# A decoder layer on one core: TensorE in source order through the gates, attention scores in pairs, and the adaLN sums placed elsewhere

## The chip, the core and the metric

One core of a Trainium2 chip runs the whole layer in one launch. The metric is the time of one execution in microseconds of the device. The core's engines work side by side and meet through semaphores: TensorE (PE in the profile, with PEld for its weight loads) multiplies, VectorE (DVE) and ScalarE (ACT) do element-wise work, GpSimd (POOL) a little of both, and SyncE (SP) issues the loads. Results of TensorE land in eight PSUM banks.

## The reference, cut to what matters

SEQ is 256, D_MODEL 1024, D_FF 2816, 8 heads of 64, SSM width 512. With 256 tokens there is a single MoBA block, so the attention is plain causal attention with ALiBi.

```python
ada = jax.nn.silu(c) @ w_ada[l] + b_ada[l]                # nine vectors of 1024
sh1, sc1, g1, sh2, sc2, g2, sh3, sc3, g3 = jnp.split(ada, N_ADA, axis=-1)
h = modulate(rmsnorm(x, norm_ffn1[l]), sh1, sc1)
x = x + 0.5 * g1[:, None, :] * swiglu(h, w_ffn1_in[l], w_ffn1_out[l])
h = modulate(rmsnorm(x, norm_mix[l]), sh2, sc2)
q, k, v, u, ga, gs = jnp.split(h @ w_in[l], IN_SPLITS, axis=-1)
y_att = moba_attention(q.reshape(hd), k.reshape(hd), v.reshape(hd))
y_ssm = s5_mixer(u, ...)       # diagonal complex state space, then gelu and a sigmoid gate (w_glu)
merged = (jax.nn.sigmoid(ga) * (y_att @ w_br_att[l]) + jax.nn.sigmoid(gs) * (y_ssm @ w_br_ssm[l]))
x = x + g2[:, None, :] * (merged @ w_out[l])
h = modulate(rmsnorm(x, norm_ffn2[l]), sh3, sc3)
x = x + 0.5 * g3[:, None, :] * swiglu(h, w_ffn2_in[l], w_ffn2_out[l])
return rmsnorm(x, norm_final)
```

All inputs are float32, and each weight is read once.

## The kernel before

**Weights.** Every weight matrix comes in units of 1 MB: `add_unit` and its kin list them, and SyncE's queue loads them in the order of that list into a ring `raw` of four slots (`NRAW`). The load of unit i is issued when unit i-4 has been used up. A weight unit is split in two quanta of 128x1024; ScalarE rounds a quantum to `w_hi` (L296), VectorE makes the rest, `w_lo` (L304), and a 128x128 block then takes three 256-column matmuls: hi x hi, hi x lo, lo x hi (`mm3` L327 to L329, `proj_mm` L500 to L502, and L649 in the start). A quantum is 24 matmuls. The splits run `AHEAD` = 4 quanta ahead of TensorE, in five buffers.

**The adaLN vectors.** The nine vectors v = 0 to 8 take four units each from the same ring. VectorE multiplies each half by silu(c) and adds it to `acc` (`consume_ada`, L274 and L276, two instructions a unit). When the fourth unit is in, `ada_done` queues `do_cols` on `pe_fill`, which runs four quanta later: column sums over the partitions on TensorE (L403, a 32-wide column group for each quarter), a copy to `ada_rows` by ScalarE (L408), two small matmuls with columns of the identity that turn the rows to columns (L410), and `ada_cols` on VectorE. `fill` takes one due item from `pe_fill` for each quantum. Vector 2, 4 and 3 are spread through FFN1 (`ffn_units`, one unit where `put * room < total * (n + 1)`), 5, 7 and 6 through the mixer by `MIX_ADA` (one unit behind each of the last 12 of its 14 weight units), 8 in FFN2.

**Stages of TensorE** (times of the profile): the start and the first seven FFN1 tiles to 64, FFN1 to 233, norm, q, k and v to 263, four u tiles to 274, the mixer's gates to 360, SSM gate, branches and output projection to 416, FFN2 to 600. `ssm_prep`, a generator that is advanced once a quantum in FFN1, builds the SSM's tables, with groups of four 128x128 transposes in banks 2 and 3 by turns (L896, L910, L935).

**The gates stage.** Each of the 16 gate tiles takes one quantum: 24 matmuls with the tile's bank out of 4, 5 and 6 by turns, then ScalarE's tanh. Between tiles `events` list the other work: for each head the scores `qk_mm` (L1272, L1273) with the softmax of VectorE and ScalarE behind it, one tile later `p_t` (three transposes, L1306), another tile later `pv_mm` (L1325, L1327; it does two heads at a time, in column groups 0 to 63 and 64 to 127 of one bank). `s_mm(0)` and `s_mm(1)` (L1188, 16 matmuls of 64 columns each) make the SSM's inputs from `U`, which is copied out of the u tiles' banks in 64 small copies, half of them on VectorE (L1180). The scans follow on VectorE, and `y_mm` (L1246, twelve matmuls at once, in column groups of 32) makes their outputs between the matmuls of gate 6 and later.

**What sets the order.** Some stages have TensorE's order written out (`manual_schedule`). From the u tiles through the gates a scheduler sets it by its own estimates: it may pull single instructions of the events between the matmuls of a tile. On the other engines it sets the order in any case.

**The final gain.** `final_gain` turns the last norm's gain from rows to a column with an 8x8 transpose (L1438), 30 quanta into what follows the first raw pair of FFN2.

## Time and profile before

| | us |
|---|---|
| three runs | 611.45, 613.01, 613.42 (median 613.01) |
| the profiled execution | 611.65 |
| its span in the trace | 609.5 |
| TensorE busy | 598.2 |
| VectorE busy | 456.1 |
| ScalarE busy | 326.9 |

The profile is that of one execution. Times in rows count from the start of its span; 2.15 us of the execution lie outside the span. A matmul's row has its start and its duration from issue to drained end; matmuls overlap, so what one costs in a stream is the distance between two starts. "PEclk" is the granted share of TensorE's full clock.

### The profile page before, as it was taken

The numbers are of one execution on the slowest core, as the hardware profiler recorded it, in microseconds if no ns is written. First come the engines' busy times: TensorE is split into PE (matmuls) and PEld (weight loads), VectorE is DVE, ScalarE is ACT, GpSimd is POOL, SyncE is SP. The second block draws the span as 40 slices with busy tenths as digits, with TensorE's granted clock in tenths as the row PEclk, the third lists the DMA queues.
The fourth block names the chain that finished last, engine by engine and source line by source line (L and its number), as shares of the span: only waits on it lengthen the run. The fifth ranks groups of instructions, "written<-read, shape, count | busy, mean of one in ns | idle before, by whom it ended". The sixth has DMA issues, their size and how long they took to land.

```text
span 609.5 us, 12820 instructions
## 1 busy us (share of the span) xinstructions
PE 598.2 (98%) x5328; PEld 571.3 (94%) x5328; DVE 456.1 (75%) x838; ACT 326.9 (54%) x537; POOL 25.3 (4%) x37
## 2 busy tenths in 40 slices
PE   7999999999999999999999999999999999999996
PEld 7888999999999999998987899999999999999995
DVE  2689999889867569998999859968975646445433
ACT  4445856469435445846536865447744444444434
POOL 6201010020000001000000000001000000000000
PEclk8999999999999999998999999999999999999997
DMA  9999989875969555888448836564586746745201
GB/s 278 335 312 247 362 276 368 280 263 177 317 212 343 178 172 172 312 270 284 139 140 282 276 135 208 195 221 139 208 275 209 247 168 233 249 149 200 70 2 70
DMA packets 97770, 136.70 MB, mean 224 GB/s; under 512 B 7761, under 2 KB 77474, under 8 KB 97712
## 3 DMA queue, kind: packets, MB, share of 16 engines
q1 hardware_dynamic: 97424, 135.81, 66.8%
q8 instruction: 42, 0.69, 0.5%
q14 instruction: 16, 0.13, 0.1%
q0 software_dynamic: 288, 0.07, 0.1%
HBM read 134.82 MB, written 1.05 MB: 223 GB/s over the span
## 4 chain that ended last, share of the span: by engine, by line
PE 88%; DVE 4%; DMA 4%; ACT 2%; issue 1%; POOL 0%; SPq 0%; ACTq 0%; DVEq 0%
PE bank L327 16%; PE bank L328 16%; PE bank L329 16%; PE bank L500 8%; PE bank L501 8%; PE bank L502 8%; PE bank L649 5%; DVE w_lo L304 2%; PE bank L425 1%; DMA raw<-in_w_in_dram 1%; PE bank L1246 1%; DMA raw<-in_w_ada_dram 1%; PE bank L1188 1%; DMA ssm_G<-in_w_ffn_in_dram 1%; DVE acc L276 1%
## 5 line engine op out<-in xcount | busy, mean ns | idle before, releaser
L304 DVE TENSOR_TENSOR w_lo<-raw,w_hi 128x1024 fp32r<-128x1024 f32 x168 | 204.2, 1223 | 84.2 <-ACT w_hi L296 83.8
L296 ACT CAST w_hi<-raw 128x1024 fp32r<-128x1024 f32 x168 | 174.0, 1048 | 165.5 <-PE bank L328 97.4
L327 PE MATMUL bank<-h_hi,w_hi 128*128 128x256 f32 x736 | 209.5, 285 | 0.0
L329 PE MATMUL bank<-h_hi,w_lo 128*128 128x256 f32 x736 | 207.1, 281 | 0.0
L328 PE MATMUL bank<-h_lo,w_hi 128*128 128x256 f32 x736 | 207.0, 281 | 0.0
L327 PEld LDWEIGHTS bank<-h_hi,w_hi 128*128 128x128 f32 x736 | 139.5, 190 | 3.9 <-issue 2.3
L329 PEld LDWEIGHTS bank<-h_hi,w_lo 128*128 128x128 f32 x736 | 140.0, 190 | 0.3 <-issue 0.2
L328 PEld LDWEIGHTS bank<-h_lo,w_hi 128*128 128x128 f32 x736 | 139.0, 189 | 0.1
L500 PE MATMUL bank<-a,w_hi 128*128 128x256 f32 x352 | 99.2, 282 | 0.0
L501 PE MATMUL bank<-a,w_hi 128*128 128x256 f32 x352 | 98.9, 281 | 0.0
L502 PE MATMUL bank<-a,w_lo 128*128 128x256 f32 x352 | 98.4, 280 | 0.0
L276 DVE SCALAR_TENSOR_TENSOR acc<-raw,csil,acc 128x1024 f32<-128x1024 f32 x49 | 62.8, 1281 | 7.8 <-DMA raw<-in_w_ada_dram 7.5
L500 PEld LDWEIGHTS bank<-a,w_hi 128*128 128x128 f32 x352 | 66.5, 189 | 1.0 <-issue 1.0
L502 PEld LDWEIGHTS bank<-a,w_lo 128*128 128x128 f32 x352 | 66.7, 190 | 0.0
L501 PEld LDWEIGHTS bank<-a,w_hi 128*128 128x128 f32 x352 | 66.1, 188 | 0.0
L327 PE MATMUL bank<-a,w_hi 128*128 128x258 f32 x112 | 31.9, 286 | 0.0
L328 PE MATMUL bank<-a,w_hi 128*128 128x258 f32 x112 | 31.8, 284 | 0.0
L329 PE MATMUL bank<-a,w_lo 128*128 128x258 f32 x112 | 31.5, 282 | 0.0
L649 PE MATMUL bank<-h_hi,w_hi 128*128 128x256 f32 x112 | 27.4, 294 | 0.9 <-ACT w_hi L296 0.5
L649 PE MATMUL bank<-h_lo,w_hi 128*128 128x256 f32 x112 | 27.8, 286 | 0.0
L649 PE MATMUL bank<-h_hi,w_lo 128*128 128x256 f32 x112 | 27.4, 283 | 0.0
L446 POOL TENSOR_TENSOR rstd<-rstd,mhalf 128x2 f32<-128x2 f32 x4 | 4.7, 1168 | 456.8 <-DVE rstd L445 456.8
(337 smaller groups left out, 893.0 us busy)
## 6 DMA issues: line engine op xcount, KB each, us to landing
raw<-in_w_ffn_in_dram SPq DMA_DIRECT2D x36, 1024.0 KB, 5.4
raw<-in_w_ada_dram SPq DMA_DIRECT2D x28, 1024.0 KB, 5.2
raw<-in_w_ffn_out_dram SPq DMA_DIRECT2D x22, 1024.0 KB, 5.3
raw<-in_w_in_dram SPq DMA_DIRECT2D x16, 1024.0 KB, 5.5
raw<-in_w_ada_dram SPq DMA_DIRECT2D x16, 512.0 KB, 8.1
raw<-in_w_out_dram SPq DMA_DIRECT2D x4, 1024.0 KB, 4.8
a<-in_w_ffn_in_dram SPq DMA_DIRECT2D x8, 448.0 KB, 7.1
ssm_G<-in_w_ffn_in_dram SPq DMA_DIRECT2D x4, 896.0 KB, 10.7
```

Of the source, the lines that this page charges most:

```text
L276: nc.vector.scalar_tensor_tensor(out=a, in0=r[:, k, :], scalar=cs, in1=a, op0=ALU.mult, op1=ALU.add)
L296: nc.scalar.copy(hi, r)
L304: nc.vector.tensor_tensor(out=lo, in0=r, in1=hi.bitcast(F32), op=ALU.subtract)
L327: nc.tensor.matmul(o, st[0], mv[0], start=first, stop=False)
L328: nc.tensor.matmul(o, st[0], mv[1], start=False, stop=False)
L329: nc.tensor.matmul(o, st[1], mv[0], start=False, stop=last)
L425: nc.tensor.matmul(p[q:q + 32, 0:256], csil[:, k, :], r[:, k, :], start=(k < 4), stop=(k >= 4), tile_position=(0, q))
L500: nc.tensor.matmul(mm3_o, wj[0], a[0], start=first and j % 2 == 0, stop=False)
L501: nc.tensor.matmul(mm3_o, wj[0], a[1], start=False, stop=False)
L502: nc.tensor.matmul(mm3_o, wj[1], a[0], start=False, stop=last and j % 2 == 1)
L649: nc.tensor.matmul(pb[b][:, n * S:(n + 1) * S], z[:, b * 128:(b + 1) * 128], h[hl][:, kb, :], start=(kb == 0 and n == 0 and y == 0), stop= ...
L1188: nc.tensor.matmul(S_b[f][n][:, i * 64:(i + 1) * 64], ssm["G"][n][:, 8 * f + i, :], U[:, 8 * f + i, 0:NC4], start=True, stop=True,)
```

## The change

Five things are changed.

1. **Units of `ada`.** Vector 5 joins FFN1: its 16 units are put so that the first half of the stage gets six and the second half ten, one for each weight unit. In the mixer, vector 7's four units stand behind k and u units, none behind the first four gate units, and vector 6's four behind the last four.
2. **Finishing a vector.** `do_cols` becomes `sums` (column sums, copy to `ada_rows`), then one quantum later `turn_rows` (two full 128x128 transposes instead of the two matmuls with identity columns; VectorE picks the columns it needs), then two quanta later a `spacer`, one 8x8 transpose whose result nobody reads. One more spacer stands ahead of the u tiles.
3. **TensorE's order** from the u tiles to the last gate is that of the source. `s_mm(0)` stands behind the third u tile, `s_mm(1)` behind gate 2. `y_mm` begins at gate 8.
4. **Paired scores.** `qk_mm` does two heads, on partitions 0 to 63 and 64 to 127, in banks 0 and 6, at gates 2, 5, 8 and 11; `p_t` of both follows at gates 5, 8, 11, 14 in banks 1 and 7, `pv_mm` at 7, 10, 13, 15. Gate tiles use banks 4, 5, 7 and 1 for the first four and 4 and 5 by turns from then on.
5. **Smaller moves.** `final_gain` comes 8 quanta in, not 30. `ssm_prep` starts one quantum later and uses bank 2 alone.

```diff
--- before.py
+++ after.py
@@ -31,7 +31,7 @@
 AHEAD = 4
 FILL_DELAY = 4
 PUMP = 1
-MIX_ADA = (0, 0, 1, 1, 1, 1, 1, 1, 1, 1, 1, 1, 1, 1)
+MIX_ADA = (0, 0, 1, 1, 1, 1, 0, 0, 0, 0, 1, 1, 1, 1)
 HOLD = 3
 RAWS = 2
 KTILES = 7
@@ -180,12 +180,14 @@
         total, put, room = len(spread), 0, len(units) - 5
         for n, u in enumerate(units):
             u()
-            while put < total and put * room < total * (n + 1):
+            while put < total and put * room < (
+                total * (n + 1) if total < 16 else max(12 * (n + 1), 20 * (n + 1) - 4 * room)
+            ):
                 ada_unit(*spread.popleft())
                 put += 1
 
-    ffn_units(T["w_ffn1_in"][0], T["w_ffn1_out"][0], KTILES, [(v, j) for v in (2, 4, 3) for j in range(4)])
-    mix_ada = deque((v, j) for v in (5, 7, 6) for j in range(4))
+    ffn_units(T["w_ffn1_in"][0], T["w_ffn1_out"][0], KTILES, [(v, j) for v in (2, 4, 3, 5) for j in range(4)])
+    mix_ada = deque((v, j) for v in (7, 6) for j in range(4))
 
     def mix_sprinkle(n=1):
         for _ in range(n):
@@ -385,19 +387,26 @@
 
     def ada_cols(v, p, ks):
 
-        o, b = ada[v][:, ks], bada[:, v, ks]
+        o, b, g = ada[v][:, ks], bada[:, v, ks], norm_cols[v][:, ks] if v in norm_cols else None
+        if len(p.shape) == 3:
+            o, b, g = (z if z is None else z.rearrange("p (q n) -> p q n", n=2) for z in (o, b, g))
         if v in norm_cols:
             nc.vector.scalar_tensor_tensor(out=o, in0=p, scalar=1.0, in1=b, op0=ALU.add, op1=ALU.add)
-            nc.vector.tensor_tensor(out=o, in0=o, in1=norm_cols[v][:, ks], op=ALU.mult)
+            nc.vector.tensor_tensor(out=o, in0=o, in1=g, op=ALU.mult)
         else:
             nc.vector.tensor_tensor(out=o, in0=p, in1=b, op=ALU.add)
             if v % 3 == 2:
                 nc.vector.tensor_scalar(o, o, 0.5, None, op0=ALU.mult)
 
+    def spacer():
+
+        p = bank(state["bank"])
+        nc.tensor.transpose(p[:, 0:8], rows[0], ident[0:8, 0:8])
+
     def ada_done(v):
         a = acc.pop(v)
 
-        def do_cols():
+        def sums():
             p = bank(state["bank"])
             for q in range(4):
                 nc.tensor.matmul(
@@ -406,13 +415,16 @@
                 )
             rs = sb("ada_rows", [128, 256])
             nc.scalar.copy(rs, p[:, 0:256])
+            pe_fill.appendleft((state["q"] + 1, lambda: turn_rows(rs)))
+
+        def turn_rows(rs):
+            p = bank(state["bank"])
             for n in range(2):
-                nc.tensor.matmul(
-                    p[:, 256 + n:264:2], rs[:, n * 128:(n + 1) * 128], ident[:, ::32], start=True, stop=True
-                )
-            ada_cols(v, p[:, 256:264], slice(0, KD))
-
-        pe_fill.append((state["q"] + FILL_DELAY, do_cols))
+                nc.tensor.transpose(p[:, n * 128:n * 128 + 128], rs[:, n * 128:(n + 1) * 128], ident)
+            ada_cols(v, p[:, 0:256].rearrange("p (n q c) -> p q n c", n=2, q=4)[:, :, :, 0], slice(0, KD))
+            pe_fill.append((state["q"] + 2, spacer))
+
+        pe_fill.append((state["q"] + FILL_DELAY, sums))
 
     block_sb = {}
 
@@ -889,9 +901,10 @@
         prep_ok[0] = False
         yield
         yield
+        yield
         Cc = pcs[1]
         for i in range(2):
-            p = bank(3)
+            p = bank(2)
             for j in range(4):
                 nc.tensor.transpose(
                     p[:, j * 128:(j + 1) * 128], c_raw[i][:, j].rearrange("p a b -> p (a b)"), ident
@@ -905,7 +918,7 @@
         G = [sb(f"ssm_G{i}", [128, 16, 128]) for i in range(2)]
         for i in range(2):
             for q in range(4):
-                p = bank(2 + q % 2)
+                p = bank(2)
                 for n in range(4):
                     nc.tensor.transpose(
                         p[:, n * 128:(n + 1) * 128],
@@ -916,7 +929,7 @@
                 )
                 yield
         ssm["G"] = G
-        p = bank(3)
+        p = bank(2)
         for j in range(4):
             for n in range(2):
                 for q in range(4):
@@ -1163,6 +1176,20 @@
     for t in range(2):
         nc.scalar.copy(vt[t], vb[t])
 
+    S_b = {}
+
+    def s_mm(f):
+        S_b[f] = (bank(2), bank(3))
+        for i in range(8):
+            for n in range(2):
+                nc.tensor.matmul(
+                    S_b[f][n][:, i * 64:(i + 1) * 64], ssm["G"][n][:, 8 * f + i, :],
+                    U[:, 8 * f + i, 0:NC4], start=True, stop=True,
+                )
+
+    pe_fill.appendleft((0, spacer))
+    gates = ExitStack()
+    gates.enter_context(tc.manual_schedule(engines={E_.PE}))
     U = sb("ssm_U", [128, 16, NC4 + 1])
     nc.gpsimd.memset(U[:, :, 0:1], 0.0)
     for j in range(4):
@@ -1178,17 +1205,9 @@
                     nc.scalar.copy(o, i_)
                 else:
                     nc.vector.tensor_copy(o, i_)
-
-    S_b = {}
-
-    def s_mm(f):
-        S_b[f] = (bank(2), bank(3))
-        for i in range(8):
-            for n in range(2):
-                nc.tensor.matmul(
-                    S_b[f][n][:, i * 64:(i + 1) * 64], ssm["G"][n][:, 8 * f + i, :],
-                    U[:, 8 * f + i, 0:NC4], start=True, stop=True,
-                )
+        if j == 2:
+            s_mm(0)
+
 
     Xs = {}
 
@@ -1265,12 +1284,16 @@
     ya = []
     pv_b = {}
 
-    def qk_mm(hd):
-        j, o = hd // 2, 64 * (hd % 2)
-        p = bank(0)
-        sc_b[hd] = p
-        nc.tensor.matmul(p[:, 0:128], qT[o:o + 64, j, 0:128], kT[o:o + 64, j, 0:128], start=True, stop=True)
-        nc.tensor.matmul(p[:, 128:384], qT[o:o + 64, j, 128:256], kT[o:o + 64, j, :], start=True, stop=True)
+    def qk_mm(j):
+
+        for i in range(2):
+            sc_b[2 * j + i] = bank(6 * i)
+        for c, r in ((slice(0, 128), slice(0, 128)), (slice(128, 384), slice(128, 256))):
+            for i in range(2):
+                o = 64 * i
+                nc.tensor.matmul(
+                    sc_b[2 * j + i][:, c], qT[o:o + 64, j, r], kT[o:o + 64, j, 0:r.stop], start=True, stop=True
+                )
 
     def softmax(hd):
         p = sc_b.pop(hd)
@@ -1301,7 +1324,7 @@
 
     def p_t(hd):
         e = pn.pop(hd)
-        p = bank(1)
+        p = bank((1, 7)[hd % 2])
         for n in range(3):
             nc.tensor.transpose(p[:, n * 128:(n + 1) * 128], e[:, n * 128:(n + 1) * 128], ident)
         t = sb(("silu", "act_f")[hd % 2], [128, 384])
@@ -1330,7 +1353,6 @@
             nc.scalar.copy(ya[0][:, j, :], pp)
             nc.vector.tensor_tensor(out=ya[1][:, j, :], in0=pp, in1=ya[0][:, j, :].bitcast(F32), op=ALU.subtract)
 
-    s_mm(0)
     sg = [scan(0), scan(1)]
     gt = [sb(f"ssm_G{i}", [128, KD, S]) for i in range(2)]
 
@@ -1340,31 +1362,34 @@
     def at(n, f, *a):
         events.setdefault(n, []).append((f, a))
 
-    for hd in range(8):
-        n = 2 * hd - (hd > 6)
-        at(n, qk_mm, hd)
-        at(n, softmax, hd)
-        at(n + 1, p_t, hd)
-        at(n + 2, pv_mm, hd)
+    at(2, s_mm, 1)
     for n in range(3):
         at(n, lambda: next(sg[0], None))
         at(n + 2, lambda: next(sg[1], None))
-    at(1, s_mm, 1)
+    for j in range(4):
+        for i in range(2):
+            at(3 * j + 5, p_t, 2 * j + i)
+            at(min(3 * j + 7, 15), pv_mm, 2 * j + i)
+    for j in range(4):
+        at(3 * j + 2, qk_mm, j)
+        for i in range(2):
+            at(3 * j + 2, softmax, 2 * j + i)
     narrow = deque((f, m) for f in range(2) for m in range(8))
-    at(12, gelu, 0)
-    at(13, gelu, 1)
+    at(11, gelu, 0)
+    at(14, gelu, 1)
     for n in range(16):
         g, j = divmod(n, 8)
-        p = bank(4 + n % 3)[:, 0:S]
+        p = bank((4, 5, 7, 1)[n] if n < 4 else 4 + n % 2)[:, 0:S]
         hi, lo = nextq()
         for k in range(KD):
             mm3(p, (hi[:, k, :], lo[:, k, :]), hk(h, k), k == 0, k == KD - 1)
-            if n > 5 and k % 3 == 1 and narrow:
+            if n > 7 and k % 3 == 1 and narrow:
                 y_mm(*narrow.popleft())
         nc.scalar.activation(gt[g][:, j, :], p, AF.Tanh, scale=0.5)
         for f, a in events.get(n, []):
             f(*a)
         fill()
+    gates.close()
     yy = (sb("h_hi", [128, KD, S], F32R), sb("h_lo", [128, KD, S], F32R))
     yh = [y[:, 0:4, :] for y in yy]
     ys = [y[:, 4:8, :] for y in yy]
@@ -1438,7 +1463,7 @@
         nc.tensor.transpose(p[:, 0:KD], rows[0], ident[0:8, 0:8])
         nc.vector.tensor_copy(nf, p[:, 0:KD])
 
-    pe_fill.append((state["q"] + 30, final_gain))
+    pe_fill.append((state["q"] + 8, final_gain))
 
     def each(g):
         if g == 0:
```

Three places show how this stands in TensorE's order. First, TensorE behind the u tiles, before. `bank_3605` is the fourth u tile's, `bank_3640` that of the sums of vector 5, `bank_3667` takes `s_mm(0)`, `bank_3687` is the first gate's.

```order
L329 MATMUL bank_3605<-h_hi,w_lo 128x256
L403 MATMUL bank_3640<-acc,ones 32x256 x4
L1188 MATMUL bank_3667<-ssm_U,ssm_G_1398 128x64 x4
L410 MATMUL bank_3640<-ident,ada_rows 128x4 x2
L1188 MATMUL bank_3667<-ssm_U,ssm_G_1398 128x64 x2
L327 MATMUL bank_3687<-h_hi,w_hi 128x256
L328 MATMUL bank_3687<-h_lo,w_hi 128x256
L329 MATMUL bank_3687<-h_hi,w_lo 128x256
```

The same place after, on TensorE: `bank_3599` is the third u tile's, `bank_3662` the fourth's, `bank_3644` and `bank_3645` take `s_mm(0)`, of whose 16 matmuls the last six are shown.

```order
L1185 MATMUL bank_3644<-ssm_U,ssm_G_1428 128x64
L1185 MATMUL bank_3645<-ssm_U,ssm_G_1429 128x64
L1185 MATMUL bank_3644<-ssm_U,ssm_G_1428 128x64
L1185 MATMUL bank_3645<-ssm_U,ssm_G_1429 128x64
L1185 MATMUL bank_3644<-ssm_U,ssm_G_1428 128x64
L1185 MATMUL bank_3645<-ssm_U,ssm_G_1429 128x64
L329 MATMUL bank_3662<-h_hi,w_hi 128x256
L330 MATMUL bank_3662<-h_lo,w_hi 128x256
L331 MATMUL bank_3662<-h_hi,w_lo 128x256
```

`s_mm(0)` moved ahead of the fourth u tile, whole, and the finishing of a vector no longer stands in the middle of it.

Second, TensorE in a late gate, before. `bank_4353` is a gate tile's, `bank_4419` takes one head's scores, `bank_4167` its transposes, `bank_4252` two heads' outputs, `bank_4174` a vector's sums.

```order
L1306 MATMUL bank_4167<-ident,at_e 128x128
L328 MATMUL bank_4353<-h_lo,w_hi 128x256
L1306 MATMUL bank_4167<-ident,at_e 128x128 x2
L329 MATMUL bank_4353<-h_hi,w_lo 128x256
L1246 MATMUL bank_4238<-a_3851,big_1882 32x64 x4
L1246 MATMUL bank_4238<-a_3851,big_1883 32x64 x4
L1246 MATMUL bank_4238<-ssm_U,ssm_L 32x64 x4
L1272 MATMUL bank_4419<-kT,qT 128x128
L1325 MATMUL bank_4252<-act_f,v_3381 64x256
L403 MATMUL bank_4174<-acc,ones 32x256 x4
L1327 MATMUL bank_4252<-silu,v_3382 64x128
L1327 MATMUL bank_4252<-act_f,v_3382 64x128
```

After, TensorE behind gate 5 (`bank_3961`): `bank_3998` and `bank_4005` take the transposes of two heads, `bank_4012` and `bank_4013` the scores of the next two.

```order
L330 MATMUL bank_3961<-h_lo,w_hi 128x256
L331 MATMUL bank_3961<-h_hi,w_lo 128x256
L1329 MATMUL bank_3998<-ident,at_e 128x128 x3
L1329 MATMUL bank_4005<-ident,at_e 128x128 x3
L1294 MATMUL bank_4012<-kT,qT 128x128
L1294 MATMUL bank_4013<-kT,qT 128x128
L1294 MATMUL bank_4012<-kT,qT 128x256
L1294 MATMUL bank_4013<-kT,qT 128x256
L329 MATMUL bank_4042<-h_hi,w_hi 128x256
L330 MATMUL bank_4042<-h_lo,w_hi 128x256
```

What was spread over the matmuls of several tiles stands between two tiles, both heads together.

Third, TensorE in FFN2's second half, where vector 8 is finished, before.

```order
L502 MATMUL bank_5654<-a_6573,w_lo 128x256
L500 MATMUL bank_5655<-a_6573,w_hi 128x256
L410 MATMUL bank_6759<-ident,ada_rows 128x4 x2
L501 MATMUL bank_5655<-a_6573,w_hi 128x256
L502 MATMUL bank_5655<-a_6573,w_lo 128x256
```

After, TensorE at the spacer of that vector, 48 matmuls behind its two transposes (L423).

```order
L330 MATMUL bank_6858<-h_lo,w_hi 128x256
L331 MATMUL bank_6858<-h_hi,w_lo 128x256
L404 MATMUL bank_6888<-ident,rows_96 128x8
L329 MATMUL bank_6858<-h_hi,w_hi 128x256
L330 MATMUL bank_6858<-h_lo,w_hi 128x256
```

An 8x8 transpose is now the last break ahead of the rest of FFN2, where L410 was.

## Rows read from the trace of the kernel before

**Rows 1.** The page: TensorE's busy time first; bandwidth in 40 slices of 15.2 us.

```profile
PE 598.2 (98%) x5328; PEld 571.3 (94%) x5328; DVE 456.1 (75%) x838; ACT 326.9 (54%) x537; POOL 25.3 (4%) x37
...
GB/s 278 335 312 247 362 276 368 280 263 177 317 212 343 178 172 172 312 270 284 139 140 282 276 135 208 195 221 139 208 275 209 247 168 233 249 149 200 70 2 70
```

**Rows 2.** Windows: length, busy time (records) of each engine, granted clock, DMA.

```profile
194.00:234.00 40.00, 40.00 (x341) 40.00 (x341) 25.90 (x43) 19.71 (x28) 0.00 (x0) 1.00 0.51 169
...
360.00:416.00 56.00, 56.00 (x478) 56.00 (x476) 45.30 (x74) 29.33 (x44) 0.00 (x0) 1.00 0.52 176
440.00:496.00 56.00, 56.00 (x478) 56.00 (x477) 35.43 (x35) 23.95 (x26) 0.00 (x0) 1.00 0.68 230
497.00:534.00 37.00, 37.00 (x329) 37.00 (x328) 21.68 (x20) 16.71 (x19) 0.00 (x0) 1.00 0.69 228
537.00:593.00 56.00, 56.00 (x477) 55.94 (x475) 26.61 (x29) 21.46 (x25) 0.00 (x0) 1.00 0.31 107
```

**Rows 3.** TensorE's timeline at the final gain: start, duration, instruction.

```profile
496.21 0.28 PE L329 MATMUL bank<-h_hi,w_lo 128*128 128x256 f32 x1
496.42 0.22 PE L1438 MATMUL bank<-ident,rows 8*128 8x8 f32 x1
...
496.80 0.28 PE L328 MATMUL bank<-h_lo,w_hi 128*128 128x256 f32 x1
```

**Rows 4.** TensorE's timeline where vector 8 is finished in FFN2.

```profile
536.24 0.28 PE L500 MATMUL bank<-a,w_hi 128*128 128x256 f32 x1
536.35 0.50 PE L410 MATMUL bank<-ident,ada_rows 128*128 128x4 f32 x4
...
536.92 0.28 PE L502 MATMUL bank<-a,w_lo 128*128 128x256 f32 x1
```

**Rows 5.** TensorE's timeline at four transposes of the SSM's tables in FFN1.

```profile
115.97 0.60 PE L910 MATMUL bank<-ident,big 128*128 128x128 f32 x4
116.33 0.37 PE L500 MATMUL bank<-a,w_hi 128*128 128x256 f32 x1
```

**Rows 6.** TensorE's timeline at one head's scores, between gate matmuls.

```profile
302.08 0.49 PE L1272 MATMUL bank<-kT,qT 64*128 64x128 f32 x2
...
302.93 0.39 PE L327 MATMUL bank<-h_hi,w_hi 128*128 128x256 f32 x1
303.15 0.28 PE L328 MATMUL bank<-h_lo,w_hi 128*128 128x256 f32 x1
```

**Rows 7.** TensorE's timeline at the `pv` matmuls of the last two heads.

```profile
357.04 0.43 PE L1325 MATMUL bank<-silu,v 128*64 128x256 f32 x1
357.05 0.43 PE L1325 MATMUL bank<-act_f,v 128*64 128x256 f32 x1
...
357.84 0.42 PE L403 MATMUL bank<-acc,ones 128*32 128x256 f32 x4
```

**Rows 8.** TensorE's timeline between u tiles and gates; in brackets the wait and its releaser.

```profile
274.32 0.64 PE L403 MATMUL bank<-acc,ones 128*32 128x256 f32 x8
274.89 1.11 PE L1188 MATMUL bank<-ssm_U,ssm_G 128*128 128x64 f32 x8
276.81 0.61 PE L410 MATMUL bank<-ident,ada_rows 128*128 128x4 f32 x4 [0.81 <-ACT ada_rows L408]
```

**Rows 9.** Lines of VectorE, 258 to 360: busy time, mean ns of one, idle before.

```profile
L304 DVE TENSOR_TENSOR w_lo<-raw,w_hi 128x1024 fp32r<-128x1024 f32 x25 | 30.4, 1222 | 2.4 <-ACT w_hi L296 2.2
L276 DVE SCALAR_TENSOR_TENSOR acc<-raw,csil,acc 128x1024 f32<-128x1024 f32 x18 | 23.1, 1281 | 0.2
L1180 DVE COPY ssm_U<-bank 32x64 f32<-32x64 f32 x32 | 7.1, 222 | 1.6 <-ACT ssm_U L1178 1.0
```

**Rows 10.** VectorE's timeline: the first copies of `U`.

```profile
269.01 0.45 DVE L1180 COPY ssm_U<-bank 32x64 f32<-32x64 f32 x2
```

**Rows 11.** Window at the first gates, columns as in rows 2.

```profile
277.50:281.50 4.00, 4.00 (x23) 4.00 (x23) 3.79 (x10) 2.01 (x6) 0.00 (x0) 0.57 0.98 349
```

**Rows 12.** SyncE's queue: first issue and length of the row of four loads.

```profile
356.63 19.41 SPq L261 DMA_DIRECT2D raw<-in_w_out_dram  x4
```

## The prediction

> **What bounds the kernel now.** I read the busy line of the page first, then TensorE's stretches, then its instructions one by one at the places that the change touches. TensorE is busy for 598.2 of 609.5 us [rows 1], and in the long stretches for all of their time [rows 2]. So waits are hardly what can be won. What can be won is on TensorE itself: fewer records, cheaper records, or records that follow each other faster. The windows show that the last is open. Take stretches that hold hardly anything but 256-column matmuls: 341 records in 40 us (194 to 234), 478 in 56 us (360 to 416 and 440 to 496) and 477 in 56 us (537 to 593), against 329 in 37 us (497 to 534) [rows 2]. A window counts also the two or three records that overlap its edges; without them 440 to 496 runs at 118 ns a matmul and 497 to 534 at 113.5 ns. The granted clock is 1.00 in all, the shape is the same, and TensorE doesn't idle. So this stream has **two paces, 4.5 ns apart**.
>
> What sets the pace? From 440 on it is slow until a single 8x8 transpose at 496.42; the fast pace begins right behind that [rows 3]. It stays until the `ada` work near 536, and is slow behind L410 [rows 4]. I read the whole trace in this way: a pace is kept from one break (instructions that are no 256-column matmul) to the next. After a break that ends with a small tile, such as the 8x8 transpose, it is fast about 4 times in 5; after four full transposes of the SSM tables 12 times in 13; after L410 nearly always slow. That is a statistic of some forty breaks, with no mechanism shown; I price with it and make its failure a rival.
>
> **The change, part by part.** All sums stand against the profiled execution: 611.65 us, 609.5 of them the span. It is the second fastest of the four times at hand (611.45, 613.01, 613.42 beside it).
>
> *Spacers and the moved final gain.* One 8x8 transpose lengthens the way from 496.21 to 496.80 to 0.59 us, where two steps of 0.118 would have done: it costs 0.36 [rows 3]. L410 costs, by the same sum, 0.68 less 0.24, thus 0.44 [rows 4]. The two full transposes that take its place come to about 0.22: four stand in 0.36, 0.09 each [rows 5], and a little for the edges. So each finished vector pays 0.36 for its spacer and gets 0.22 back from its turn, 0.14 net. What returns by the pace:
> In the last stretch the spacer stands two quanta (48 matmuls) behind the turn; of 477 some 429 remain, x 4.5 ns x 0.8 = 1.5, net **-1.4**. In FFN2's first part the final gain comes 22 quanta earlier and costs what it cost before; 456 matmuls x 4.5 ns x 0.8, **-1.6**. Between gates and output projection the spacer stands some 130 matmuls in; 340 x 4.5 ns x 0.8 less 0.14, **-1.1**. In FFN1 the slow stretch from 194 gains on the 264 matmuls behind the last spacer, 0.95; the breaks of the added vector put stretches at risk that are fast now (+0.5); four spacers cost 1.44, three turns return 0.66, and the added vector costs 0.57 for its column sums (274.32 to 274.89 [rows 8]) and 0.22 for its turn: **+1.1**. The group: -3.0, with bounds of -6 if every spacer works and +2 if none does.
>
> *Score pairs.* One head takes from 302.08 to 303.15, less one step: 0.96 us [rows 6], eight heads 7.7. The diff issues two heads together, on row groups 0 to 63 and 64 to 127 and in two banks. No row of before shows two row groups at once; the nearest is two column groups: the `pv` matmuls of two heads start 10 ns apart, and both are through from 357.04 to 357.84 [rows 7]. By that row a pair costs what a head costs and some 0.1 more: 4 x 1.05 = 4.2, a gain of 3.5. If they don't overlap, only edges go, 4 x 0.1 = 0.4. I take **-3.5**, range -0.4 to -3.7. By the Trainium skill, page "TensorEngine Tiling (Array Packing)", Key Properties, tiles of different row groups load and multiply in parallel; the sum by that is the 3.5 too, and no row here shows it.
>
> *Fewer breaks in the gates.* In the scheduled order transposes, `pv`, column sums and scores stand mixed between matmuls. By my count of both orders the stream of gate matmuls resumes 40 times between the column sums behind the u tiles and those behind the last gate, and 25 times now; four of the 15 are in the score pairs already. A break costs about 0.2 before any work of its own: some 0.1 at its start, and 0.11 at its end, where the first matmul takes 0.22 (302.93 to 303.15) for 0.113 [rows 6]. That is 11 x 0.2 = 2.2. Three of four `pv` pairs are split by other work before and stand together now, some 0.4 each. Together **-3.5**, range -2 to -5.
>
> *Sums moved out of the gates.* One vector less is finished here, 0.57 and 0.44: **-1.0**; two turns for L410 give **-0.4**. Since no L410 stands in the middle of s_mm(0), its wait of 0.81 goes [rows 8], and behind it the time at the lower clock (1.2 GHz): the granted clock averages 0.57 in 277.5 to 281.5, so 0.43 x 4 = 1.7 [rows 11]. **-2.5**.
>
> *Waits that the source order adds.* s_mm(0) now stands behind u tile 2, one tile earlier: 274.32 less a tile of 2.83 (24 steps of 0.118) and plus the spacer, about 271.8. Without a wait its 32 records, 0.112 apart (eight of them with their drain take 1.11 [rows 8]), would be through 3.6 later, at 275.4. It needs the U copies of tiles 0 and 1; VectorE begins them at 269.0 [rows 10], and in its new order three w_lo of 1.22 and 18 copies of 0.22 [rows 9] stand up to the last of them: 276.9, and s_mm(0) ends at 277.5: **+2.1**, between 0 and 6 (copies as late as in before, behind more of VectorE's work). Queued behind on TensorE are u tile 3 and every gate, which only lengthens VectorE's lead. Such a hole can bring the lower clock again: **+1.1**, between 0 and 3.4. The first transposes of probabilities stand in line behind a softmax that VectorE, full until the scans are through, delivers late: **+1.9**, 0 to 4. Two spacers, against what they win between the gates: **+0.3**.
>
> Gates: -3.5 - 3.5 - 1.0 - 0.4 - 2.5 + 2.1 + 1.1 + 1.9 + 0.3 = -5.5. With -3.0 outside **-8.5**: 603.1 against the profiled run, 604.5 against the median; I take 603.7 between. SP: the small load of the final gain now waits for the spacer behind the gates, and the last of four loads of w_out queues behind it, which was issued at 375.7, 16.1 us behind the last gate [rows 12]; the spacer comes some 124 matmuls of 0.118, 14.6 us, behind that gate. So nothing slips; if the spacer came later than that, the load would slip by as much, under the four quanta (11.3 us) that TensorE has in hand.
>
> **The rivals.**
>
> *A: the pace does not follow the spacer.* For it: my case for the final gain is a single one, and some breaks broke the pattern. Then the group outside the gates costs some 1.9 in place of giving 3.0: 608.6. [...]
>
> *B: in-order waits eat the gates.* TensorE can't step past a late copy or a late softmax, as the scheduled order did. For it: VectorE's load in this stretch. At their upper ends two of the three waits alone (6 and 3.4, with the third at 1.2) make 10.6 in place of 5.1, and the gates give nothing: 609.2.
>
> *C: the scores of a pair run one behind the other.* 3.1 less gain: 606.8.
>
> *D, slower: FFN1 runs dry.* Its second half now carries ten units of `ada` beside ten of weights. A weight unit lasts 48 matmuls, 5.6 us; so 20.97 MB in 56 us, 375 GB/s. The loads of the similar mix at 277.5 delivered 349 [rows 11], the page's best slice 368 [rows 1]. VectorE would have 2 x 1.22 + 2 x 1.28 = 5.0 of each 5.6 us taken [rows 9] ahead of its evacuations. TensorE's lead is four quanta, 11.3 us: it decides for this case when the loads come under 20.97 / 67.3 = 312 GB/s. At 263, a loaded slice in the same FFN1 [rows 1], they need 79.7 us, 12.4 too many: 616. Against it: at the best rates shown the shortfall is 1 to 4 us, inside the lead, and units without `ada` follow.
>
> **How the numbers follow.** The forecast has 0.53, A 0.17, B 0.15, C 0.08, D 0.07. The forecast's own range is 599 to 606.5. A and C reach 608.6, B 609.2, with a us for the difference between runs 610.5; D lies outside, and under 598.5 only all lower bounds at once would lead. A measurement of this kernel tells 0.3%, 1.8 us, from no change. Faster by more: nearly all of the forecast and C, most of A and B, 0.86. Same: the upper ends of A and B and a mild D, 0.08. Slower: D, and B with the lower clock for the whole of its bound, 0.06.
>
> **What would show it.** Right: about 495 records in place of 477 or 478 in 56 us of FFN2 and the output projection; a pair of heads through in some 1.1 us; no wait for `ada_rows` near the first gate; a wait for `ssm_U` of 2 to 5 us in s_mm(0), and of about 2 at the first transposes of `at_e`. Wrong: 118 ns a matmul behind spacers (A); TensorE idle or at the lower clock for over 8 us between 270 and 300 (B); the second head's scores starting where the first's end (C); waits for w_hi or w_lo between 150 and 235 (D).

## The result

The changed kernel takes 608.52 us (median of 20 runs, 605.93 to 612.94), the kernel before 611.84 (20 runs, 609.84 to 616.01). The ratio is 0.9945, 95% interval 0.9928 to 0.9962: faster by 3.3 us, where the forecast of 603.7 is 8.1 below this median of before (9.3 below its first one). The time lies above the forecast's own range (599 to 606.5) and inside that of the rivals (to 610.5), and the gain is less than half of the forecast. Of the runs further down two are slow ones, one of them 959.34 us at a mean clock of 0.562; no ratio counts them.

The profiled execution of the changed kernel took 606.88 us, 604.3 of them its span, and its view of the cores, for before and after, shows the clock that TensorE had on average:

```profile
core 0: 609.5 us, clock 0.988
...
core 0: 604.3 us, clock 0.989
```

That execution is one of the quicker ones. The 20 runs of the changed kernel had mean clocks of 0.977 to 0.990 and were mostly the longer, the lower: (1 - clock) x span has the median 8.5 us there and 5.5 us in 23 runs of before. Take that off each run, and 599.5 us remain after and 606.2 before. So in the middle the change wins 6.6 us of time at full clock and pays 3.0 of it back at the lower one. That sum counts every stretch at the lower clock. In both profiled executions some 3.5 us of it lie in the last 8, where TensorE finishes; in the gates it is 3.4 after and 1.7 before, and at the start 0 after and 1.7 before (8 of the 18 profiled executions here have such a stretch near 11 or 26 us). So where the 3.0 of the middle run are paid, the profiles show only in part.

Where the time went in the two profiled executions, by the starts of the same weight matmul (of the 4272 with 256 columns) in both traces:

| stretch | forecast, us | measured, us |
|---|---|---|
| start | 0 | -0.4 |
| rest of FFN1 | +1.1 | +1.3 |
| norm, q, k, v | 0 | 0.0 |
| u tiles and gates | -5.5 | -0.5 |
| SSM gate to output projection | -1.1 | -1.5 |
| FFN2, first part | -1.6 | -2.2 |
| FFN2, last part | -1.4 | -1.9 |
| sum | -8.5 | -5.2 |

Everything outside the gates came within 0.2 us of the forecast or better. The windows of the changed kernel, columns as in [rows 2]:

```profile
194.00:234.00 40.00, 40.00 (x352) 39.31 (x351) 25.99 (x42) 20.26 (x29) 0.00 (x0) 1.00 0.51 174
360.00:416.00 56.00, 56.00 (x489) 55.85 (x488) 46.22 (x78) 30.77 (x46) 0.25 (x1) 1.00 0.52 175
440.00:496.00 56.00, 56.00 (x496) 56.00 (x495) 35.66 (x34) 24.79 (x28) 0.00 (x0) 1.00 0.70 235
```

352, 489 and 496 records where 341, 478 and 478 were: these stretches run at 113.3 ns now, the second from its spacer at 373 on. The gates did not come as forecast. TensorE's waits from 262 to 360, before and then after (total, times, longest):

```profile
PE bank L410 <- ACT ada_rows L408: 0.8, 1, 0.8
```

```profile
PE bank L1185 <- DVE ssm_U L1207: 2.2, 2, 1.6
PE bank L1329 <- DVE at_e L1320: 1.4, 2, 1.0
PE bank L329 <- DVE ssm_U L1207: 1.2, 1, 1.2
```

The timeline of s_mm(0) in the changed kernel, and the windows of this place:

```profile
272.45 1.06 PE L1185 MATMUL bank<-ssm_U,ssm_G 128*128 128x64 f32 x8
275.09 0.63 PE L1185 MATMUL bank<-ssm_U,ssm_G 128*128 128x64 f32 x4 [1.58 <-DVE ssm_U L1207]
276.31 4.41 PE L1185 MATMUL bank<-ssm_U,ssm_G 128*128 128x64 f32 x20 [0.59 <-DVE ssm_U L1207]
```

```profile
272.40:276.40 4.00, 1.83 (x15) 1.62 (x15) 3.75 (x13) 3.09 (x11) 0.00 (x0) 1.00 1.09 349
276.40:283.60 7.20, 7.20 (x36) 7.20 (x37) 5.69 (x16) 1.64 (x8) 0.00 (x0) 0.53 0.79 265
```

TensorE has work for 1.83 of 4 us, and then runs at a granted clock of 0.53, almost its level of 1.2 GHz, for 7.2 us: 3.4 us lost, twice what [rows 11] show of before.

### The profile page after: what moved, and what is told of

Same layout as the page of the kernel before. It is cut to its first block, busy times and chain, and to the rows that moved or that the text cites. A ratio compares the mean times of both kernels' runs of the same rounds, so it can differ in the third digit from the quotient of the medians.

```text
span 604.3 us, 12801 instructions
## 1 busy us (share of the span) xinstructions
PE 586.4 (97%) x5322; PEld 560.6 (93%) x5322; DVE 455.8 (75%) x838; ACT 325.1 (54%) x536; POOL 25.8 (4%) x37
## 4 chain that ended last, share of the span: by engine, by line
PE 73%; DVE 11%; DMA 6%; issue 3%; ACT 3%; SPq 2%; POOL 0%; POOLq 0%; DVEq 0%; ACTq 0%
PE bank L329 15%; PE bank L330 14%; PE bank L331 14%; PE bank L512 7%; PE bank L513 7%; PE bank L514 7%; DVE w_lo L306 3%; PE bank L661 2%; DMA raw<-in_w_ada_dram 2%; DVE acc L278 2%; DMA raw<-in_w_ffn_in_dram 1%; ACT w_hi L298 1%; DMA a<-in_w_ffn_in_dram 1%; PE bank L1185 1%; PE bank L1265 1%
## 5 line engine op out<-in xcount | busy, mean ns | idle before, releaser
L330 PE MATMUL bank<-h_lo,w_hi 128*128 128x256 f32 x736 | 204.3, 278 | 0.0
L331 PE MATMUL bank<-h_hi,w_lo 128*128 128x256 f32 x736 | 204.2, 278 | 0.0
L512 PE MATMUL bank<-a,w_hi 128*128 128x256 f32 x352 | 98.4, 280 | 0.0
L513 PE MATMUL bank<-a,w_hi 128*128 128x256 f32 x352 | 97.7, 277 | 0.0
L661 PE MATMUL bank<-h_lo,w_hi 128*128 128x256 f32 x112 | 27.6, 285 | 0.0
L661 PE MATMUL bank<-h_hi,w_lo 128*128 128x256 f32 x112 | 27.2, 282 | 0.0
## 6 DMA issues: line engine op xcount, KB each, us to landing
ssm_G<-in_w_ffn_in_dram SPq DMA_DIRECT2D x4, 896.0 KB, 10.2
```

The costliest lines, as they stand in the source:

```text
L330: nc.tensor.matmul(o, st[0], mv[1], start=False, stop=False)
L331: nc.tensor.matmul(o, st[1], mv[0], start=False, stop=last)
L512: nc.tensor.matmul(mm3_o, wj[0], a[0], start=first and j % 2 == 0, stop=False)
L513: nc.tensor.matmul(mm3_o, wj[0], a[1], start=False, stop=False)
L661: nc.tensor.matmul(pb[b][:, n * S:(n + 1) * S], z[:, b * 128:(b + 1) * 128], h[hl][:, kb, :], start=(kb == 0 and n == 0 and y == 0), stop= ...
```

## The experiments

**Turns, spacers and the final gain alone.** `e4_before_spacer` is the kernel before with the new `ada_done` (turn and spacer) and the final gain 8 quanta in, which is the line shown.

```diff
-    pe_fill.append((state["q"] + 30, final_gain))
+    pe_fill.append((state["q"] + 8, final_gain))
```

> The kernel before with only the new way to finish a vector (sums, two transposes, spacer) and the final gain 8 quanta in; gates, scores and placing of the sums as before. Theory (pace): the stretches 194 to 234, 360 to 416, 440 to 496 and 537 to 593 run at 113.3 ns, some 1600 x 4.6 ns x 0.8 = 5.9 us, less six times 0.14: about 5 us faster than before, 607 us, 0.992. Rival (the pace does not follow): 1 us slower than before, 1.001.

Measured: 604.65 us, ratio 0.9894 (0.9873 to 0.9915). These parts of the change alone win 7 us, twice the whole change. Its windows:

```profile
194.00:234.00 40.00, 40.00 (x349) 39.85 (x348) 26.51 (x44) 20.95 (x28) 1.59 (x1) 1.00 0.50 156
360.00:416.00 56.00, 56.00 (x492) 55.85 (x490) 46.50 (x77) 31.07 (x46) 0.74 (x1) 1.00 0.54 179
440.00:496.00 56.00, 56.00 (x497) 56.00 (x496) 35.16 (x32) 24.89 (x28) 0.00 (x0) 1.00 0.71 238
```

**The change without spacers.** `e1_no_spacer` takes all spacers out and puts the final gain back to 30 quanta.

```diff
-            pe_fill.append((state["q"] + 2, spacer))
...
-    pe_fill.appendleft((0, spacer))
...
-    pe_fill.append((state["q"] + 8, final_gain))
+    pe_fill.append((state["q"] + 30, final_gain))
```

> The changed kernel without its spacers, and with the final gain 30 quanta in as before. Theory (the pace follows the last break, so a spacer pays): the 264 matmuls at the end of FFN1, some 360 up to the output projection, some 450 of FFN2's first part and 412 of its last run at 118 instead of 113.3 ns, 4.6 ns x 1490 = 6.8 us lost, six spacers of 0.36 saved: 4.5 us slower than the changed kernel, about 613 us or a ratio to before of 1.002. Rival (the pace does not follow the spacer): 2 us faster than the changed kernel, about 606.5 us or 0.991.

Measured: 610.94 us, 0.999 (0.9969 to 1.001), 2.4 slower than the changed kernel, between the two. The windows say why:

```profile
194.00:234.00 40.00, 40.00 (x355) 39.46 (x354) 25.89 (x40) 19.44 (x29) 0.00 (x0) 1.00 0.60 199
360.00:416.00 56.00, 56.00 (x493) 55.27 (x494) 45.58 (x76) 31.12 (x49) 0.00 (x0) 1.00 0.56 188
440.00:496.00 56.00, 56.00 (x478) 56.00 (x477) 35.49 (x35) 24.57 (x28) 0.00 (x0) 1.00 0.71 238
```

Only 440 to 496, where the final gain now stands behind the stretch, is slow again (478 records). The others are fast without a spacer: the two full transposes of the turn had set that. So the pace does follow the last break, but a turn in place of L410 is worth most of it. Part of the 2.4 us is clock: with (1 - clock) x span taken off each run, e1 has 600.9 us and the change 599.5, so spacers and final gain are worth about 1.4. `e16_late5_no_spacer` repeats this where few waits disturb: `e12_sched_late5` (below) without its spacers, the final gain left at 8.

> e12_sched_late5 (scheduler's order, vector 5 late, 600.8 us) without its spacers; the final gain stays 8 quanta in. Theory from e1_no_spacer (the pace follows the last break, and the two full transposes of a turn set the fast one by themselves): the stretches at 194, 360 and 537 stay at 113.3 ns, six spacers of 0.36 go, 1 to 2.5 us faster: 598.5 to 600 us, ratio to before 0.979 to 0.981. Rival (it was chance in e1_no_spacer, and a turn leaves the slow pace in 2 of 3 places): 0.5 to 3 us slower, 601 to 604 us, 0.983 to 0.988.

Measured: 601.9 us, 0.9833 (0.9809 to 0.9857) against 0.9827: no difference. Three long stretches are fast behind a turn, but the one from 360 to 416 is slow, which costs what the spacers save:

```profile
360.00:416.00 56.00, 56.00 (x477) 55.97 (x475) 47.89 (x76) 29.41 (x42) 1.61 (x1) 1.00 0.57 189
```

Neither theory holds alone. Of the stretches of 100 and more such matmuls, all 89 behind an 8x8 transpose run at the fast pace in the eighteen traces, and of those behind a turn (e1 and e16) seven of nine. What makes the difference is not shown.

**Source order or the scheduler's.** `e5_scheduled` leaves TensorE's order in the gates to the scheduler and keeps all else.

```diff
-    gates.enter_context(tc.manual_schedule(engines={E_.PE}))
```

> The changed kernel with TensorE's order from the u tiles to the last gate left to the scheduler again; sums, spacers, pairs and their places as in the change. Theory (TensorE in source order can't step past late copies and a late softmax, and each such wait is followed by a stretch at the lower clock): the waits of 4.9 us in the gates fall to under 2, time at the lower clock goes from 8.5 us in the middle of the runs to that of before, 5.5, and work that is split again costs back 1 to 2: 3 to 4 us faster than the changed kernel, 604.5 to 605.5 us, ratio to before 0.989 to 0.991. Rival (the order is not to blame): 608 to 609 us, 0.994 to 0.996.

Measured: 601.34 us, 0.9846 (0.9824 to 0.9867), faster than the theory had it. This one line costs the change 7 us. Its waits from 262 to 360, and its window at s_mm(0):

```profile
PE bank L1328 <- DVE at_e L1319: 1.1, 1, 1.1
PE bank L412 <- DVE a L724: 0.6, 1, 0.6
PE bank L1185 <- DVE ssm_U L1206: 0.6, 1, 0.6
```

```profile
276.40:283.60 7.20, 7.20 (x64) 7.20 (x64) 6.35 (x16) 4.20 (x14) 0.00 (x0) 1.00 0.84 271
```

64 records where the changed kernel does 36, at full clock. The two orders differ mainly in three things: the scheduler spreads s_mm(0) through the fourth u tile, puts the column sums of vector 7 two whole tiles later (48 matmuls behind that u tile, not right behind it), and the transposes of probabilities of the first two pairs 4 to 21 matmuls later (a gate has 24).

**Which of the three.** Seven kernels keep source order and move what stands too early, one place after the other.

`e2_smm_tile3` and `e3_smm_gate0` put s_mm(0) whole behind the fourth u tile and behind the first gate.

```diff
-        if j == 2:
+        if j == 3:
             s_mm(0)
```

```diff
-        if j == 2:
-            s_mm(0)
...
+    at(0, s_mm, 0)
     at(2, s_mm, 1)
```

> The changed kernel with s_mm(0) behind the fourth u tile instead of the third. Theory (the gates' gain is spent on the wait for the copies of U in s_mm(0) and on the lower clock behind it): TensorE arrives 2.8 us later, the waits of 1.7 and 0.75 us in s_mm(0) shrink to under 0.5, and less than half of the 3.4 us at the lower clock remains: 3 to 4.5 us faster than the changed kernel, 604 to 605.5 us, ratio to before 0.987 to 0.990. Rival (VectorE's backlog is the bound there): the wait comes back at the next place that needs VectorE, gate 2 or the first transposes of probabilities, and the time stays at 608 us, 0.994.

> The changed kernel with s_mm(0) behind the first gate, 5.7 us of matmuls later than in the change. Theory (wait and lower clock come from the place of s_mm(0)): no wait in s_mm(0), no time at the lower clock, 4 to 6 us faster than the changed kernel, 602.5 to 604.5 us, 0.985 to 0.988. Rival (VectorE's backlog): scans and softmax begin 3 to 5 us later, the first transposes of probabilities wait 3 us longer, and the gain is 2 us or less, 606.5 us or more, 0.991.

Measured: 610.08 us, 0.9983 (0.9968 to 0.9997), and 606.03 us, 0.9917 (0.9895 to 0.9938). The hole, TensorE's idle stretch, moved, and e2 is slower than either text expected. In e2 s_mm(0) waits for ScalarE's copy of vector 7's sums, which stand in one of its banks (ScalarE has copies of `U` and a w_hi ahead of it), and then the softmax is late; in e3 it is the softmax, for longer (the longest waits):

```profile
PE bank L1185 <- ACT ada_rows L417: 3.2, 1, 3.2
PE bank L1329 <- DVE at_e L1320: 2.9, 1, 2.9
```

```profile
PE bank L1327 <- DVE at_e L1318: 4.2, 2, 4.1
```

`e10_gate0_late_pt` is e3 with the first two heads' transposes at gate 7 and their outputs at gate 8.

```diff
-            at(3 * j + 5, p_t, 2 * j + i)
-            at(min(3 * j + 7, 15), pv_mm, 2 * j + i)
+            at(3 * j + 5 if j else 7, p_t, 2 * j + i)
+            at(min(3 * j + 7, 15) if j else 8, pv_mm, 2 * j + i)
```

> Source order with s_mm(0) behind the first gate as in e3_smm_gate0, and the first two heads' transposes two gates later (gate 7, their outputs at gate 8). Theory (each hole in TensorE's stream costs its length and then a stretch at the lower clock): the one hole left in e3_smm_gate0, 4.2 us at these transposes, and the 3.4 us of lower clock behind it go: 6 us faster than e3_smm_gate0's 606, 600 to 601.5 us, 0.981 to 0.984. Rival (the softmax is late by more than that, or the late heads collide with the next pair): half or less of it, 603.5 to 606 us, 0.987 to 0.991.

Measured: 606.63 us, 0.9939 (0.9918 to 0.9959): no gain on e3. The rival, with a time 0.6 us above its range: the second pair's transposes, at gate 8, now wait for their softmax and for the bank of the first pair's outputs:

```profile
PE bank L1327 <- DVE at_e L1318: 3.1, 1, 3.1
PE bank L1327 <- DVE ssm_Pi L1352: 3.0, 1, 3.0
```

`e9_smm_split` writes the scheduler's spreading of s_mm(0) by hand.

```diff
-            tile_b(p, nextq(), h, KD)
+        if j < 3:
+            tile_b(p, nextq(), h, KD)
+        else:
+            s_mm(0, (0, 1))
+            hi, lo = nextq()
+            for k in range(KD):
+                mm3(p, (hi[:, k, :], lo[:, k, :]), hk(h, k), k == 0, k == KD - 1)
+                s_mm(0, {2: (2,), 4: (3, 4, 5, 6), 7: (7,)}.get(k, ()))
```

> The changed kernel, TensorE in source order as in the change, but s_mm(0) written in four pieces through the fourth u tile (4, 2, 8 and 2 of its 16 matmuls ahead of it and behind its 9th, 15th and 24th matmul), nearly as the scheduler put them in e5_scheduled. The transposes of probabilities stay where the change has them. Theory 1 (s_mm(0) in one piece makes the hole and the lower clock): TensorE waits under 1 us in this stretch, the lower clock there goes, and the time comes within 1.5 us of e5_scheduled: 601 to 603 us, ratio to before 0.984 to 0.987. Theory 2 (the first transposes, which wait for the softmax ahead of the next scores, carry half of it): 604.5 to 606.5 us, 0.989 to 0.992.

Measured: 609.55 us, 0.9975 (0.9948 to 1.0001). Both theories missed. s_mm(0) hardly waits now, and one long hole stands at vector 7's column sums, the second of the three:

```profile
PE bank L412 <- DVE a L724: 6.4, 1, 6.4
PE bank L1186 <- DVE ssm_U L1215: 0.5, 1, 0.5
```

The sums go to PSUM bank 3, and VectorE must first have read s_mm(0)'s result there. Its timeline in e9 shows that the reads (L724, those that name a bank) stand between the copies of `U`; the last of bank 3 ends at 285.6:

```profile
279.15 0.69 DVE L724 TENSOR_TENSOR a<-ssm_Pr,bank 128x512 f32<-128x512 f32 x1 [0.45 <-PE bank L1186]
279.76 0.68 DVE L724 TENSOR_TENSOR a<-ssm_Pi,bank 128x512 f32<-128x512 f32 x1
280.47 0.94 DVE L1215 COPY ssm_U<-bank 32x64 f32<-32x64 f32 x4
281.44 1.23 DVE L306 TENSOR_TENSOR w_lo<-raw,w_hi 128x1024 fp32r<-128x1024 f32 x1
...
284.86 0.69 DVE L724 TENSOR_TENSOR a<-ssm_Pr,bank 128x512 f32<-128x512 f32 x1
```

VectorE of e5 does the same at the same times, within 0.7 us. There TensorE does the first two gates meanwhile, and waits 0.6 us for this read.

`e13_split_bank1` is e9 with these sums in bank 1.

```diff
+    state["bank"] = 1
     gates = ExitStack()
```

> e9_smm_split (source order, s_mm(0) in four pieces, 609.6 us) with one number changed: the column sums and turn of vector 7, which come behind the fourth u tile, go to PSUM bank 1 instead of bank 3, which holds s_mm(0)'s result until VectorE has read it. Theory (a chain of holes, each where the order lets TensorE meet VectorE's backlog between 274 and 290): the wait of 6.4 us at the sums goes and with it the 3.4 us of lower clock; what is left are waits of 0.5 to 1 us and the softmax: 601 to 603.5 us, ratio to before 0.983 to 0.987. Rival (VectorE's backlog meets TensorE at the next place in any source order: s_mm(1), whose banks are free only when the scans' first products are made, or the first transposes): the wait comes back there with 3 us or more, and the time is 605 to 608 us, 0.990 to 0.995.

`e14_split_bank1_pt6` is e13 with the first pair's transposes behind gate 6, `e15_split_bank1_ptall` moves those of the second and third pair by a gate too (its line is shown).

```diff
-            at(3 * j + 5, p_t, 2 * j + i)
+            at((6, 9, 12, 14)[j], p_t, 2 * j + i)
```

> e13_split_bank1 (source order, s_mm(0) in pieces, vector 7's sums in bank 1, 607.5 us) with the transposes of the first two heads one gate later, behind gate 6, as the scheduler has them. Theory (three places in the source order meet VectorE's backlog, and the hole goes to the next as long as one is left): the wait of 3.8 us at these transposes becomes about 1 us, no stretch at the lower clock is left in the gates, and source order comes to e5_scheduled's time: 601 to 603 us, ratio to before 0.983 to 0.987. Rival (a wait comes back at the outputs of these heads or at the next pair, one gate behind): 605 to 607 us, 0.990 to 0.993.

> e14_split_bank1_pt6 (607.9 us) with the transposes of the second and third pair of heads one gate later as well (gates 9 and 12 instead of 8 and 11). Theory (every hole left is a place where the fixed order meets a softmax or an evacuation that is late by less than a gate): the two waits of 1.7 and 1.9 us at the second pair and the 3.4 us at the lower clock behind them go, nothing longer than 1.5 us is left: 601 to 603.5 us, ratio to before 0.983 to 0.987. Rival (a hole comes back still further on, at the outputs of these heads or at y_mm): 605 to 608 us, 0.989 to 0.994.

Measured: e13 607.5 us, 0.9934 (0.9914 to 0.9954); e14 607.91, 0.9941 (0.9921 to 0.9962); e15 603.87, 0.9869 (0.9844 to 0.9895). The rival named the place twice: the hole goes on to the first transposes in e13 and to the second pair's in e14 (1.6 us at 317.7 and 1.8 at 320.0; its time is 0.9 above the rival's range). In e15 no wait over 1.3 us is left, and its time is 0.4 above the theory's range. The waits of e13, then of e15:

```profile
PE bank L1336 <- DVE at_e L1327: 3.8, 2, 3.6
PE bank L329 <- DVE ssm_U L1216: 1.3, 1, 1.3
PE bank L1186 <- DVE ssm_U L1216: 0.5, 1, 0.5
```

```profile
PE bank L329 <- DVE ssm_U L1216: 1.3, 1, 1.3
PE bank L1355 <- ACT act_f L1339: 0.6, 1, 0.6
PE bank L1186 <- DVE ssm_U L1216: 0.5, 1, 0.5
PE bank L1336 <- DVE at_e L1327: 0.4, 1, 0.4
```

In e15's profiled execution, its quickest, the clock is full from 240 to 372, and its span is 599.5 against e5's 598.6. Source order with hardly anything ahead of what it waits for gives back 4.7 of the 7 us. Its other runs still lose up to 5 us more than the best (601.58 to 606.62), and what the remaining 2.5 are is not shown.

**The sums.** `e6_v5_in_mixer` puts vector 5 back, `e7_ada_early` moves vector 7 two weight units ahead, `e8_early7_late5` does that and puts vector 5 behind the last gate units.

```diff
-MIX_ADA = (0, 0, 1, 1, 1, 1, 0, 0, 0, 0, 1, 1, 1, 1)
+MIX_ADA = (1, 1, 1, 1, 0, 0, 0, 0, 0, 0, 2, 2, 2, 2)
```

(That of e8. The lists of vectors follow: in e8, as later in e12, vector 5 leaves FFN1 and the mixer has 7, 5, 6. In e6 it is that of before, with the vectors 5, 7, 6; in e7 it begins 1, 1, 1, 1 and the rest is the change's.)

> The changed kernel with the units of vector 5 back in the mixer (none of its sums in FFN1, one unit behind every one of the last 12 mixer units). Theory (the fourth vector costs FFN1 3 us, of which 1.2 is a wait for the copy of its row and the rest its own work and pace): FFN1 ends 2 to 3 us earlier; in the gates VectorE has 8 additions of 1.28 more, so waits and the lower clock there cost 2 to 5 us more: 608 to 611 us, 0.994 to 0.999. Rival (the load on VectorE in the gates is not what the waits come from): 605.5 to 606.5 us, 0.990 to 0.992.

> The changed kernel with the four units of vector 7 two weight units earlier (behind the four q and k units instead of the k and u units), nothing else. Theory (the waits come from VectorE's backlog ahead of the copies of U): two units, 5.1 us of additions, go from in front of the copies to where VectorE has time; the waits of 2.3 us in s_mm(0) shrink below 0.5, gate 2's wait of 1.2 goes, time at the lower clock falls from 8.5 to 5 or less: 4 to 6 us faster than the changed kernel, 602.5 to 604.5 us, 0.985 to 0.988. Rival (the place of s_mm(0) alone sets the waits, whatever VectorE has done before): within 1.5 us of the changed kernel, 607 to 609 us, 0.992 to 0.996.

> The changed kernel with vector 7's units behind the four q and k units, and vector 5 out of FFN1: its four units stand with those of vector 6 behind the last four gate units, two units each. Theory (both the fourth vector in FFN1 and the backlog at the copies cost): FFN1 2 to 3 us shorter, waits and lower clock at s_mm(0) gone, VectorE takes 8 more additions behind gate 8, where it is busy for 57%: 6 to 9 us faster than the changed kernel, 599.5 to 602.5 us, 0.980 to 0.985. Rival (three loads for each gate unit of 5.7 us can't be delivered in time): waits for w_hi or w_lo behind gate 10 of 3 to 6 us, 604 to 607 us, 0.988 to 0.993.

Measured: e6 613.98 us, 1.0045 (1.0029 to 1.0061): longer than either text expected. In source order the sums had to leave the early gates. Its two longest groups of waits from 262 to 360:

```profile
PE bank L1185 <- DVE ssm_U L1207: 5.1, 4, 1.5
PE bank L1329 <- DVE at_e L1320: 4.5, 2, 3.3
```

e7 is at 610.93 us, 0.9979 (0.9954 to 1.0004): my theory fell, and the time is above the rival's range too. The q and k units have no room either. TensorE waits for h_hi there (1.5 us), the clock falls at 258, and 3.9 us are lost from 236 to 266 before anything is won. e8 pays the same at that place and gets 2.6 us back in FFN1: 607.5 us, 0.9933 (0.9915 to 0.9951). With vector 7 where the change has it, and in the scheduler's order, the late vector 5 is `e12_sched_late5`, `MIX_ADA` ending in 2, 2, 2, 2.

> e5_scheduled with vector 5 out of FFN1; its four units stand with vector 6's behind the last four gate units, two each. Theory (the fourth vector costs FFN1 some 3 us, and VectorE has room behind gate 8): FFN1 2.5 to 3 us shorter, the gates at most 1 us longer: 598.5 to 600 us, 0.979 to 0.982, the best of all here. Rival (what FFN1 gains comes back in the late gates as waits and lower clock, as in e8_early7_late5): 601 to 604 us, 0.984 to 0.988.

Measured: 600.79 us, 0.9827 (0.9808 to 0.9845), the shortest time here. From 64 us on FFN1 is 3.2 us shorter than in e5, the gates are 1.5 and the stretch behind them 0.7 longer (profiled executions); against e5's interval the whole is no clear difference.

**The pairs.** `e11_sched_unpaired` is e5 with both matmuls of one head ahead of the other's.

```diff
-        for c, r in ((slice(0, 128), slice(0, 128)), (slice(128, 384), slice(128, 256))):
-            for i in range(2):
+        for i in range(2):
+            for c, r in ((slice(0, 128), slice(0, 128)), (slice(128, 384), slice(128, 256))):
```

> e5_scheduled (601.3 us, 0.985) with the scores of a pair in another order: both matmuls of one head, then both of the other, in the same banks and row groups and at the same places. Theory (only neighbours in different row groups overlap): the inner two of the four still overlap, so a pair costs 0.25 to 0.5 us more, 1 to 2 us in all: 602.3 to 603.3 us, 0.986 to 0.988. Rival (row groups don't overlap at all, the pair's gain comes from fewer breaks): no difference beyond 0.5 us.

Measured: 601.19 us, 0.983 (0.9812 to 0.9848), no different from e5, as the rival had it; but its reason is wrong. The timeline of the changed kernel, and of e11, at one pair:

```profile
324.17 0.93 PE L1294 MATMUL bank<-kT,qT 64*128 64x128 f32 x8
325.03 0.38 PE L329 MATMUL bank<-h_hi,w_hi 128*128 128x256 f32 x1
325.25 0.28 PE L330 MATMUL bank<-h_lo,w_hi 128*128 128x256 f32 x1
```

```profile
303.98 0.93 PE L1293 MATMUL bank<-kT,qT 64*128 64x128 f32 x8
304.84 0.39 PE L329 MATMUL bank<-h_hi,w_hi 128*128 128x256 f32 x1
```

Two heads take 0.86 us, where one took 0.85 [rows 6]. They overlap wholly, and in either order of issue: in e11's trace the second head's matmuls start 13 ns behind the first's, as in the pairs of the change 7 ns.

## Why the prediction was wrong, step by step

- **The step that failed: the waits that the source order adds, with the clock behind them.** I put s_mm(0) at +2.1, the transposes at +1.9, the lower clock at +1.1. (By its own terms the last copy of that sum is through at 276.7, not 276.9.) The profiled waits are 2.2, 1.4 and 1.2 (gate 2, which waits for a bank of the u tiles, and which I had costed at nothing): 4.8 for 4.0. The clock was further off: 3.4 us in the profiled run for 1.1, and over all runs 3.0 more than before, where I had taken a net gain of 0.6. And I treated the waits as independent prices. I read them as one backlog of VectorE, met wherever the order allows it: with places moved or freed, waits of 4.6 to 7.3 us in all stay from 262 to 360 (e2, e3, e9, e10, e13, e14), against 4.8 in the change, 2.8 in e15 and 2.3 in e5.
- **Rival B is what happened.** Its place and its time were right (609.2 for 608.5), and so was its sign: between 270 and 300 TensorE is idle for 3.4 us and at the lower clock for 6.8, 10.2 where over 8 were named. I gave it 0.15. That its price fits is in part luck: it had 10.6 us of waits and clock, where the profile has 8.2 and the gates' work is 1.9 short. The order rows showed s_mm(0) whole, and rows 9 and 10 VectorE's load; what I did not weigh is that the scheduler's order, which has these instructions later, had been hiding this backlog in the kernel before.
- **Gates without the waits: 8.1 forecast, about 6.2 measured.** In the changed kernel the stretch is 0.5 us shorter than in before; with 4.8 of waits and 3.4 of clock taken off it, and before's own 2.5, the work is 6.2 less (in e5, by the same sum, 6.3 - 2.5 + 2.3 = 6.1). The pairs gave 3.8 for 3.5 (0.97 each by the measure that gave 0.96 for a head). So the term of fewer breaks, 3.5, was some 2 too high, though 15 resumptions of the stream went, as counted (38 and 23 in the traces); which breaks cost less than 0.2 was not taken apart.
- **The sum.** Of the 3.3 us between -8.5 and -5.2 in the profiled executions, the clock makes 2.3, the waits 0.8 and the work in the gates 1.9; 1.7 came back outside the gates, where the forecast was too low.
- **The pace: right outside the gates, half right in its cause.** -4.3 for -3.0 without the start. I gave all of it to the spacer; e1 and e16 show that the turn does part of it, so the 0.36 a spacer costs is often spent for nothing.
- **Rivals A, C, D.** A's time came near, for another reason, and its mechanism is refuted by the 496 records of 440 to 496. C is refuted. D did not come: the second half of FFN1 shows no wait for w_hi or w_lo, though its fourth vector costs 3.2 us against e12.
- **Two rules beside these runs.** The Trainium skill's page "TensorEngine Tiling (Array Packing)", Key Properties, has tiles of different row groups work in parallel; the trace agrees, 0.86 us for two heads. The Trainium skill's page "TensorE: Matmul & The Clock Gate", Back-to-back issue gap, has the gap of a matmul by itself follow from columns and clock, and weight load and matmul together set it in a stream; it names no break, and these runs show two gaps, 118 and 113.3 ns, at 256 columns and full clock, by the break before.

## What to carry to other kernels

Before an order that a scheduler found is replaced by one written by hand, list each instruction of the fixed order whose operand or bank another, full engine delivers, and place it behind that engine's time; while one was early here, 4.6 to 7.3 us of waits stayed, wherever they were met. Price a hole on TensorE with the lower clock that may follow it, and look at the spread of the runs, not at one profile. And test the parts of a change one by one: here one group of parts alone gained twice the whole.
